# GpSimd's work on x, VectorE's order around the routing, and the order of eight experts in an encoder trunk

## The chip, the cores and the metric

The kernel runs on one core of a Trainium2 chip. The metric is device time in microseconds of one execution; the time before is the median of three runs. A core has TensorE (matmuls, and transposes as matmuls), VectorE, ScalarE, GpSimd and SyncE, which here issues most of the loads. They run their own instruction streams, each in order, and wait for one another by semaphores. In the profile they are PE, DVE, ACT, POOL and SP; PEld is TensorE's loading of the stationary operand, and a q behind a name is an engine's instruction queue.

## The reference, cut to what matters

```python
x = layer_norm(x, emb_ln_g, emb_ln_b)                     # x: 256 tokens x 1024, float32
for layer in range(2):
    m = mixer_block(x, ...)                               # projections, two kinds of attention, gates, output
    x = layer_norm(ALPHA * x + m, ln1_g[layer], ln1_b[layer])
    if layer == 0:
        f = swiglu(x, w_gate, w_up, w_down)               # dense, hidden width 2816
    else:                                                 # 8 experts, hidden width 3584, 2 per token
        logits = x @ w_router
        top_vals, top_idx = lax.top_k(logits, 2)
        top_w = softmax(top_vals)
        f = sum(combine[:, e:e+1] * swiglu(x, w_gate[e], w_up[e], w_down[e]) for e in range(8))
    x = layer_norm(ALPHA * x + f, ln2_g[layer], ln2_b[layer])
```

## The kernel before

**The dense part.** Activations stay on the chip, as two token tiles of 128 in `xt` and transposed in `xTh` and `xTl`. Weights come as tiles of 1 MB (`load_w`): SP issues the load into a `raw` buffer, ScalarE rounds it into `hi` (L185), VectorE subtracts to get `lo` (L192), and TensorE makes three matmuls of each product, high by high, low by high and high by low (L203 to L205). TensorE is fed from four `raw` buffers and four pairs of `hi` and `lo`.

**A seam.** Between two sub-layers a token tile is normalized (`ln_norm`, L225), transposed by TensorE and split again into high and low parts by VectorE (`to_xT`, L255 to L273); gain and bias are applied on the way to the transposed copy. The untransposed `xt`, which the next residual sum needs much later, gets its gain and bias from GpSimd (`ln_apply`, L234 and L237), in two multiplies and two adds of 1024 columns; the gain and then the bias are loaded as a broadcast into one buffer, tag `gb`. `rest` does the second token tile's transposition in the middle of the next sub-layer's first projection. In layer 0 `rest` gives back `end_norm`, the multiplies and adds for the embedding norm, called directly behind the first four projections.

**Routing.** `route(t)` is a generator in four parts for a token tile: (1) transposition, with ScalarE's high part `xth` and a low part `xtl` of the untransposed tile; (2) the router's logits; (3) ranks of the eight logits by comparisons on VectorE; (4) counts by matmul, giving each token's place (`pos`) in each expert. The router's weights `wr` stand in the `gb` buffer. `select` compares places with an iota to make a selection matrix `Sp`, and `gather` multiplies with it, on TensorE, to collect 128 token places of two experts at once into `gx`; ScalarE and VectorE copy the result out of PSUM. The second token tile's routing and the first pair's gather stand in a block in which only TensorE's order is fixed to the source's. GpSimd makes the second tile's `xtl`.

**The experts.** One at a time, in two halves of the hidden width: `gate_up` uses 16 tiles of 896 KB, `down` 7 tiles of 1 MB, raw float32, with TensorE in its 32-column blocks. A wide expert has 96 token places, a narrow one 64: three blocks or two. Down of one half runs behind gate and up of the next half; `scatter` adds an expert's weighted output to `xt`. The raw tiles rotate through 20 rooms (`rooms`), in program order. The first two experts are fixed (`FIXED = 2`, wide, loaded by constant addresses); the other six are sorted by their token counts on VectorE (`take_turns`) into the ranks of `RANK_AT`, the three largest wide, and SP reads the index from `who` ahead of an expert's loads (L1066). Experts are gathered in the pairs (0,1), (2,3), (4,5), (6,7), each pair at the end of the pair before. `cmi` (L845) says how far an expert's count goes past its places; every engine reads it into a register (L1121), and if it does, a loop at the end handles what is left over.

**What sets the order.** The program is put in order at build time by a list scheduler with its own times: on each engine the ready instruction that stands earliest in the code goes first, so later ones fill gaps. `manual_schedule(engines=...)` keeps the source's order on those engines. `issue_after(ins)` puts the instructions that its block traces on the engine of `ins` behind `ins` in issue order; it leaves other engines' instructions as they are and adds no wait for `ins` to finish. `hold_back` uses it for the next weights' splits. `warm(n)` issues n matmuls on constant data.

Of the kernel before, what the change touches and what calls it, by code (L numbers as in the profile page):

```python
# [15 lines left out]
AF = mybir.ActivationFunctionType  # L16
OP = mybir.AluOpType
# [48 lines left out]
def tile_encoder(ctx: ExitStack, tc: tile.TileContext, x_in, emb_g, emb_b, w_in, b_gate, na_rpb, sw_sink,  # L66
# [219 lines left out]
    def mixer(l, xh, xl, rest, x, mp, close_attention, early):  # L286
# [9 lines left out]
        def load_cols(c0, n):  # L296
            return [load_w(win[:, kh * 4:kh * 4 + 4, c0:c0 + n], 4, n) for kh in range(2)]
# [44 lines left out]
        if l == 0:  # L342
            with tc.manual_schedule(engines={PE, ACT, DVE}):
                end_norm = rest()
                wq = load_cols(1536, 512)
                for t in range(2):
                    proj_x(wkv, 256, t, ev_kv)
                for t in range(2):
                    proj_x(wq, 512, t, ev_q)
            end_norm()  # L350
            late_loads()
            nc.sync.dma_start(att, consts_in[:, :C_TRI])
        else:
            wq = load_cols(1536, 512)
            nc.sync.dma_start(att, consts_in[:, :C_TRI])
            for t in range(2):
                proj_x(wkv, 256, t, ev_kv)
                proj_x(wq, 512, t, ev_q, None if t else rest)
        wv = load_cols(1024, 512)
        for t in range(2):  # L360
            proj_x(wv, 512, t, ev_vna)

# [314 lines left out]
    def rest(ln, g, b):  # L677
        def part():
            out = to_xT(xt, ln, 1, *xT)
            if ln == 0:  # L680
                return lambda: ln_apply(xt, bcast(g, nc.sync), b, pool)
            hold_back(0, *out)
            ln_apply(xt, bcast(g), b, pool)
            return out[0]
        return part

# [2 lines left out]
    with tc.manual_schedule(engines={PE, ACT, DVE}):  # L689
        warm(12)  # L690
        second = ln_stats(xt[:, 1])
        to_xT(xt, 0, 0, *nxt, mid=lambda: ln_norm(xt[:, 1], second))
        warm(6)
    xT = list(nxt)
    with tc.tile_pool(name="mix0", bufs=1) as mp:
        mixer(0, *xT, rest(0, emb_g, emb_b), xt, mp, lambda ap: pools["att0"].close(), early(1))
# [25 lines left out]
    def route(t):  # L722

        tk = slice(t * 128, (t + 1) * 128)
        if not t:
            rt["xth"] = bp.tile([128, 2, D], F32R, tag="br0", name="xth")
            rt["xtl"] = bp.tile([128, 2, D], F32R, tag="br1", name="xtl")
            rt["xfull"] = xp.tile([128, KC, S], F32, tag="xTh", name="xfull")
        xth, xtl, xfull = rt["xth"], rt["xtl"], rt["xfull"]
        out = to_xT(xt, 3, t, None, None, full=xfull)  # L730
        with tc.issue_after(out.ins):
            rt[t] = act.activation(xth[:, t], xt[:, t], AF.Copy)
        (pool if t else dve).tensor_sub(xtl[:, t], xt[:, t], xth[:, t])
        yield

        ps = mm_bank()
# [2 lines left out]
            m = pe.matmul(ps[r, :128], rt["wr"][:, c], xfull[:, c, tk], start=c < 4, stop=c >= 4)  # L739
        lgT = part_tile([128, 128], "lgT")  # L740
        dve.tensor_copy(lgT, ps[:, :128])
        yield m
        ps = mm_bank()[:, :128]
        m = pe.transpose(ps, lgT, ident)
# [10 lines left out]
        dve.tensor_reduce(rank[:, t], gt, axis=AX.X, op=OP.add)  # L755
        dve.tensor_scalar(Ab[:, t], rank[:, t], 1.5, None, op0=OP.is_lt)
        dve.tensor_scalar(A[:, t], rank[:, t], 1.5, None, op0=OP.is_lt)
        yield m

        ps = mm_bank()  # L760
# [40 lines left out]

    FIXED = 2
    RANK_AT = [3, 0, 4, 1, 2, 5]
    WIDE = [True] * FIXED + [r < 3 for r in RANK_AT]

    def take_turns(comb):

# [38 lines left out]
    def gather(S_sel, n, bank=lambda c2: late_bank()):  # L848
# [15 lines left out]
        def out(c2):  # L864
            g, b = ln_col(3, 2 * c2)
            act.activation(gx[:, 2 * c2], pss[c2][:, 0], AF.Identity, bias=b, scale=g)
            g, b = ln_col(3, 2 * c2 + 1)
            dve.tensor_scalar(gx[:, 2 * c2 + 1], pss[c2][:, 1], g, b, op0=OP.mult, op1=OP.add)

        def step(c2):  # L870
            for t in range(2):
# [142 lines left out]

    def pair_select(Sp, pi, ts=(0, 1)):
        for i in range(2):
            e = 2 * pi + i
            src = turns[0] if turns else pos
            select(Sp, slice(i * 128, (i + 1) * 128), lambda t: src[:, t, e:e + 1], ts)

    def pair_start(pi):
        Sp = ep.tile([128, 2, 256], F32R, name="Sp")
        pair_select(Sp, pi)
        gx, steps, _ = gather(Sp, 256)
        return Sp, gx, steps

# [4 lines left out]

    Sp = ep.tile([128, 2, 256], F32R, name="Sp")
    gx, _, (gather_tile, gather_out) = gather(Sp, 256, acc_bank)
    with tc.manual_schedule(engines={PE}):
        steps = route(1)
        next(steps)
        next(routed)
        pair_select(Sp, 0, (0,))
        warm(4)
        next(steps)  # L1040
        gather_tile(0, 0)
        next(steps)
        for c2 in range(1, 4):
            gather_tile(c2, 0)
        warm(4)
        next(steps)
        warm(4)
        pair_select(Sp, 0, (1,))
        for c2 in range(KC // 2):
            gather_tile(c2, 1)  # L1050
            gather_out(c2)
    pair = Sp, gx, None
    ln_apply(xt, bcast(ln1_g[1]), ln1_b[1], pool)
    for t in range(2):
        pool.tensor_scalar(xt[:, t], xt[:, t], ALPHA, None, op0=OP.mult)
    new_pack()
    late = None
    ends = []
    for e in range(NE):
        Sp, gx, _ = pair  # L1060
        hs = slice(e % 2 * 128, e % 2 * 128 + 128)
        wide = WIDE[e]
        if e < FIXED:
            wg, wu, wd = mgv[:, e], muv[:, e], moe_d[0, e:e + 1]
# [5 lines left out]
        for j in range(LASTJ + 1):  # L1070
# [3 lines left out]
                    es.enter_context(tc.manual_schedule(engines={PE}))  # L1074
                h = gate_up(wg, wu, gx[:, :, hs], j, wide)
            if e == 0 and j == 1:
                comb = route_weights()
                turns += take_turns(comb)
            steps = []
            if j == LASTJ and e % 2 and e + 1 < NE:  # L1080
                pair = pair_start(e // 2 + 1)
                steps = pair[2]
            if j == 1 and ends:
# [117 lines left out]
```

## Time and profile before

| | |
|---|---|
| time before, median of 3 runs (lowest, highest) | 1434.43 us (1433.92, 1435.25) |
| the profiled execution's own time | 1437.59 us |
| its span, first to last instruction | 1435.8 us |
| busy share: TensorE, VectorE, ScalarE, GpSimd | 96%, 36%, 23%, 7% |
| mean granted clock of TensorE | 0.988 |
| bytes read from HBM | 448 MB, 313 GB/s over the span |
| GB/s in 40 slices, the first 16, then from the 18th to the 20th | 119 to 334, then 419, 419, 418 |

A timeline's row has the start and the length in us, the engine, the line, the operation, what is written from what is read with its shape, the count of merged instructions, and in brackets the idle time ahead of it and what ended it. A row of stretches has, for each engine, its busy time and (its instructions), then the granted clock as a share of 2.4 GHz, the DMA engines' busy share, and GB/s. All figures are of one execution.

### The profile page before, as it was taken

The numbers are of one execution on the slowest core, as the hardware profiler recorded it, in microseconds if no ns is written. First come the engines' busy times: TensorE is split into PE (matmuls) and PEld (weight loads), VectorE is DVE, ScalarE is ACT, GpSimd is POOL, SyncE is SP. The second block draws the span as 40 slices with busy tenths as digits, with TensorE's granted clock in tenths as the row PEclk, the third lists the DMA queues.
The fourth block names the chain that finished last, engine by engine and source line by source line (L and its number), as shares of the span: only waits on it lengthen the run. The fifth ranks groups of instructions, "written<-read, shape, count | busy, mean of one in ns | idle before, by whom it ended". The sixth has DMA issues, their size and how long they took to land. (4 is left out here: it accounts for less than half of the span.)

```text
span 1435.8 us, 26988 instructions
## 1 busy us (share of the span) xinstructions
PE 1380.6 (96%) x11875; PEld 774.8 (54%) x11875; DVE 511.5 (36%) x668; ACT 336.4 (23%) x533; POOL 100.6 (7%) x64
## 2 busy tenths in 40 slices
PE   7999999999999999899999999999999899999984
PEld 5888989999888897333333333333323233333321
DVE  8775686445677656611001101102010111101113
ACT  4566454444456653100000000000000000000000
POOL 4310030000050100500000000000000000000000
PEclk8999999999999999999999999999999999999998
DMA  8744456554474387599999999999999999999993
GB/s 292 221 131 138 153 166 228 186 195 163 152 228 145 119 334 282 205 419 419 418 405 356 374 419 417 419 420 418 418 420 418 419 419 418 419 419 419 418 419 145
DMA packets 122858, 451.24 MB, mean 314 GB/s; under 512 B 8032, under 2 KB 57568, under 8 KB 108528
## 3 DMA queue, kind: packets, MB, share of 16 engines
q1 hardware_dynamic: 120768, 442.91, 79.4%
q0 software_dynamic: 1968, 6.55, 1.6%
q8 instruction: 95, 1.56, 0.4%
q14 instruction: 27, 0.22, 0.0%
HBM read 448.38 MB, written 1.05 MB: 313 GB/s over the span
## 5 line engine op out<-in xcount | busy, mean ns | idle before, releaser
L933 PE MATMUL mm<-raw,gx 128*32 128x448 f32 x3648 | 370.2, 540 | 0.9 <-DMA raw<-in_moe_w_gate_dram 0.6
L933 PEld LDWEIGHTS mm<-raw,gx 128*32 128x32 f32 x3648 | 117.2, 110 | 224.7 <-issue 207.7
L192 DVE TENSOR_TENSOR lo<-raw,hi 128x2048 fp32r<-128x2048 f32 (+1 forms) x85 | 203.7, 2400 | 93.8 <-ACT hi L185 93.5
L962 PE MATMUL a<-raw,hT 128*32 128x512 f32 x1680 | 197.5, 594 | 12.3 <-DMA raw<-in_moe_w_down_dram 12.2
L203 PE MATMUL mm<-xTh,hi 128*128 128x256 f32 x704 | 202.3, 287 | 0.0
L205 PE MATMUL mm<-xTh,lo 128*128 128x256 f32 x704 | 200.0, 284 | 0.0
L204 PE MATMUL mm<-xTl,hi 128*128 128x256 f32 x704 | 199.6, 284 | 0.0
L933 PE MATMUL a<-raw,gx 128*32 128x448 f32 x1728 | 187.2, 540 | 0.0
L185 ACT ACTIVATE hi<-raw 128x2048 fp32r<-128x2048 f32 (+1 forms) x85 | 158.7, 1873 | 77.6 <-PE mm L204 43.2
L203 PEld LDWEIGHTS mm<-xTh,hi 128*128 128x128 f32 x704 | 134.6, 191 | 7.2 <-issue 5.4
L205 PEld LDWEIGHTS mm<-xTh,lo 128*128 128x128 f32 x704 | 134.6, 191 | 3.1 <-issue 3.1
L204 PEld LDWEIGHTS mm<-xTl,hi 128*128 128x128 f32 x704 | 134.7, 191 | 1.9 <-issue 1.5
L938 DVE TENSOR_TENSOR h<-h,mm 128x448 f32<-128x448 f32 x32 | 19.9, 621 | 303.2 <-PE mm L933 300.6
L962 PEld LDWEIGHTS a<-raw,hT 128*32 128x32 f32 x1680 | 50.8, 110 | 136.4 <-issue 102.7
L933 PEld LDWEIGHTS a<-raw,gx 128*32 128x32 f32 x1728 | 55.4, 110 | 107.5 <-issue 103.5
L937 ACT ACTIVATE h<-mm 128x448 f32<-128x448 f32 x25 | 13.6, 544 | 319.6 <-PE mm L933 319.6
L967 PE MATMUL a<-raw,hT 128*32 128x512 f32 x560 | 72.8, 592 | 0.0
L945 DVE STREAM_TRANSPOSE hT<-h 128x1344 f32<-128x1344 f32 (+1 forms) x15 | 33.6, 2240 | 106.0 <-PE a L967 54.0
L976 ACT ACTIVATE y<-a 128x512 f32<-128x512 f32 x8 | 4.8, 597 | 271.0 <-PE a L962 271.0
L1116 POOL DMA_DIRECT2D raw<-in_ln_g_dram x1 | 0.6, 602 | 774.9 <-PE mm L933 774.9
L205 PE MATMUL mm<-hi,xTl 128*128 128x256 f32 (+1 forms) x128 | 44.8, 351 | 3.4 <-DVE xTl L273 3.4
L203 PE MATMUL mm<-hi,xTh 128*128 128x256 f32 (+1 forms) x128 | 45.4, 357 | 2.3 <-DVE xTh L272 2.3
(243 smaller groups left out, 1420.6 us busy)
## 6 DMA issues: line engine op xcount, KB each, us to landing
raw<-in_moe_w_gate_dram SPq DMA_DIRECT2D x128, 896.0 KB, 17.7
raw<-in_moe_w_up_dram SPq DMA_DIRECT2D x128, 896.0 KB, 17.4
raw<-in_moe_w_down_dram SPq DMA_DIRECT2D x111, 1024.0 KB, 18.6
raw<-in_w_in_dram SPq DMA_DIRECT2D x32, 1024.0 KB, 6.4
raw<-in_ffn_w_gate_dram SPq DMA_DIRECT2D x11, 1024.0 KB, 5.4
raw<-in_ffn_w_up_dram SPq DMA_DIRECT2D x11, 1024.0 KB, 5.5
raw<-in_ffn_w_down_dram SPq DMA_DIRECT2D x11, 1024.0 KB, 5.1
raw<-in_w_out_dram SPq DMA_DIRECT2D x8, 1024.0 KB, 5.9
```

Of the source, the lines that this page charges most:

```text
L185: act.activation(hi[:, p], raw[:, p], AF.Copy)
L192: eng.tensor_sub(lo[:, p], raw[:, p], hi[:, p])
L203: pe.matmul(o, lh, rh, start=first, stop=False)
L204: pe.matmul(o, lh, rl, start=False, stop=False)
L205: pe.matmul(o, ll, rh, start=False, stop=last)
L933: pe.matmul(out[q * 32:q * 32 + 32], gx[:, c, s * 32:s * 32 + 32], wt[:, q * Q:(q + 1) * Q], start=c == 0, stop=c == KC - 1)
L937: act.activation(h[:, s, 0:Q], banks[0][s], AF.Silu)
L938: dve.tensor_mul(h[:, s, 0:Q], h[:, s, 0:Q], banks[1][s])
L945: dve.transpose(hT, h.rearrange("p s (f b) -> p s b f", f=32))
L962: pe.matmul(yb[0][r:r + 32], hT[s][:, m], w[:, n * 512:(n + 1) * 512], start=first, stop=last)
L967: pe.matmul(yb[1][r:r + 32], hT[2][:, m - 1 + i], wt[:, i, n * 512:(n + 1) * 512], start=j == 0 and m == 1, stop=last)
L976: act.activation(y[:, 0], yb[0], AF.Copy)
```

## The change

- `end_norm()` moves behind the issue of the value projection's weight loads, and so behind the loads of three constants; the warm-up there grows from 6 to 13 matmuls.
- At the seams' `ln_apply`, and at the one after the routing together with the multiplication by ALPHA, an `issue_after` is put, named after a VectorE instruction.
- In `route(1)` ScalarE's high part comes ahead of the transposition, and the low part is VectorE's in two halves, one behind the logits' copy and one behind the ranks. The block around it fixes VectorE's order as well. The warm-up ahead of the counts goes from 4 matmuls to 1.
- `FIXED` is 1, seven experts go by rank, the four largest wide. The order of widths becomes wide, narrow, wide, wide, wide, narrow, wide, narrow (before: wide, wide, narrow, wide, narrow, wide, wide, narrow). The gathered pairs become (0,0), (1,2), (3,4), (5,6), (7,7), one more than before, each gathered in an even expert's second half.
- `route_weights` and `take_turns` are put behind the last copy of the gather on VectorE.

```diff
@@ mixer
-            end_norm()
             late_loads()
...
         wv = load_cols(1024, 512)
+        if l == 0:
+            end_norm()
@@ rest
-            ln_apply(xt, bcast(g), b, pool)
+            with tc.issue_after(out[1].ins):
+                ln_apply(xt, bcast(g), b, pool)
@@
-        warm(6)
+        warm(13)
@@ route
+        def low_part(n):
+            ns = slice(n * 512, (n + 1) * 512)
+            dve.tensor_sub(xtl[:, t, ns], xt[:, t, ns], xth[:, t, ns])
+
+        if t:
+            act.activation(xth[:, t], xt[:, t], AF.Copy)
         out = to_xT(xt, 3, t, None, None, full=xfull)
-        with tc.issue_after(out.ins):
-            rt[t] = act.activation(xth[:, t], xt[:, t], AF.Copy)
-        (pool if t else dve).tensor_sub(xtl[:, t], xt[:, t], xth[:, t])
+        if not t:
+            with tc.issue_after(out.ins):
+                act.activation(xth[:, t], xt[:, t], AF.Copy)
+            low_part(0)
+            low_part(1)
...
         dve.tensor_copy(lgT, ps[:, :128])
+        if t:
+            low_part(0)
...
         dve.tensor_scalar(A[:, t], rank[:, t], 1.5, None, op0=OP.is_lt)
+        if t:
+            low_part(1)
@@
-    FIXED = 2
-    RANK_AT = [3, 0, 4, 1, 2, 5]
-    WIDE = [True] * FIXED + [r < 3 for r in RANK_AT]
+    FIXED = 1
+    RANK_AT = [4, 0, 1, 2, 5, 3, 6]
+    WIDE = [True] * FIXED + [r < 4 for r in RANK_AT]
@@ pair_select
-            e = 2 * pi + i
+            e = min(max(2 * pi - 1 + i, 0), NE - 1)
@@ the block of the second token tile
-    with tc.manual_schedule(engines={PE}):
+    with tc.manual_schedule(engines={PE, DVE}):
...
-        warm(4)
+        warm(1)
...
-            gather_out(c2)
+            gathered = gather_out(c2)
     pair = Sp, gx, None
-    ln_apply(xt, bcast(ln1_g[1]), ln1_b[1], pool)
-    for t in range(2):
-        pool.tensor_scalar(xt[:, t], xt[:, t], ALPHA, None, op0=OP.mult)
+    with tc.issue_after(gathered.ins):
+        ln_apply(xt, bcast(ln1_g[1]), ln1_b[1], pool)
+        for t in range(2):
+            pool.tensor_scalar(xt[:, t], xt[:, t], ALPHA, None, op0=OP.mult)
...
-        hs = slice(e % 2 * 128, e % 2 * 128 + 128)
+        hs = slice((e + 1) % 2 * 128, (e + 1) % 2 * 128 + 128)
...
-                comb = route_weights()
-                turns += take_turns(comb)
+                with tc.issue_after(gathered.ins):
+                    comb = route_weights()
+                    turns += take_turns(comb)
...
-            if j == LASTJ and e % 2 and e + 1 < NE:
+            if j == LASTJ and e % 2 == 0 and e + 1 < NE:
                 pair = pair_start(e // 2 + 1)
```

## Rows read from the trace of the kernel before

**Rows 1.** Stretches: busy time of PE, PEld, DVE, ACT, POOL; clock, DMA share, GB/s.
```profile
18.00:30.00 12.00, 8.67 (x38) 7.28 (x37) 11.49 (x6) 5.96 (x8) 8.37 (x5) 0.72 0.77 271
...
580.00:600.00 20.00, 16.05 (x140) 7.45 (x144) 17.75 (x52) 4.81 (x7) 14.40 (x7) 0.83 0.33 102
720.00:740.00 20.00, 20.00 (x200) 6.33 (x196) 3.10 (x2) 0.60 (x1) 0.00 (x0) 1.00 1.00 394
760.00:820.00 60.00, 60.00 (x567) 21.74 (x560) 11.14 (x19) 3.35 (x6) 0.00 (x0) 1.00 0.93 354
840.00:860.00 20.00, 20.00 (x220) 6.94 (x216) 2.11 (x2) 1.09 (x2) 0.00 (x0) 1.00 1.02 420
```

**Rows 2.** Timeline of TensorE, the last expert's down projection.
```profile
1390.54 1.92 PE L962 MATMUL a<-raw,hT 128*32 128x512 f32 x16 [0.56 <-DMA raw<-in_moe_w_down_dram]
...
1412.92 3.64 PE L962 MATMUL a<-raw 128*32 128x512 f32 x32 [0.56 <-SPq L1122]
```

**Rows 3.** Timeline of SP, the first expert's loads around its start.
```profile
591.02 0.33 SPq L199 DMA_DIRECT2D raw<-in_moe_w_gate_dram  x1
...
596.94 1.29 SPq L199 DMA_DIRECT2D raw<-in_moe_w_gate_dram  x3
```

**Rows 4.** Waits of SP, 575 to 600: us in total, times, longest.
```profile
SPq L1121 <- DVE cmi L845: 4.7, 1, 4.7
```

**Rows 5.** Timeline of TensorE: gather, first expert's start; down with gather, and without.
```profile
583.95 0.55 PE L861 MATMUL a<-Sp,xth 128*128 128x256 f32 x1 [4.25 <-DVE turn_v L830]
...
587.63 1.72 PE L933 MATMUL mm<-raw,gx 128*32 128x448 f32 x8
...
771.63 1.92 PE L962 MATMUL a<-raw,hT 128*32 128x512 f32 x16
...
787.07 1.92 PE L962 MATMUL a<-raw,hT 128*32 128x512 f32 x16
...
789.67 1.90 PE L962 MATMUL a<-raw,hT 128*32 128x512 f32 x16
```

**Rows 6.** Timeline of VectorE: routing, and the first expert's two products.
```profile
573.83 0.48 DVE L880 TENSOR_SCALAR Sp<-cst,pos 128x128 fp32r<-128x128 f32 x2
...
575.49 2.08 DVE L751 TENSOR_TENSOR eq<-lg 128x64 f32<-128x64 f32 x1
...
578.46 0.16 DVE L757 TENSOR_SCALAR A<-rank 128x8 f32<-128x8 f32 x1
...
581.18 2.62 DVE L880 TENSOR_SCALAR Sp<-cst,pos 128x128 fp32r<-128x128 f32 x2
...
598.38 0.27 DVE L839 CAST who<-turn_at 128x6 int32<-128x6 f32 x1
623.42 2.12 DVE L938 TENSOR_TENSOR h<-h,mm 128x448 f32<-128x448 f32 x3 [24.76 <-PE mm L933]
...
659.50 2.13 DVE L938 TENSOR_TENSOR h<-h,mm 128x448 f32<-128x448 f32 x3 [31.39 <-PE mm L933]
```

**Rows 7.** Timeline of GpSimd: the embedding norm's multiplies, and the routing.
```profile
17.95 5.14 POOL L234 TENSOR_TENSOR x<-x,gb 128x1024 f32<-128x1024 f32 x2 [17.02 <-DMA gb<-in_emb_ln_g_dram]
...
574.50 0.57 POOL L229 DMA_DIRECT2D gb<-in_ln_g_dram  x1 [6.13 <-PE mm L739]
575.08 2.39 POOL L733 TENSOR_TENSOR xtl<-x,xth 128x1024 fp32r<-128x1024 f32 x1
578.88 4.64 POOL L234 TENSOR_TENSOR x<-x,gb 128x1024 f32<-128x1024 f32 x2 [1.41 <-DMA gb<-in_ln_g_dram]
```

**Rows 8.** Timeline of VectorE in the first seam.
```profile
18.01 2.85 DVE L273 TENSOR_TENSOR xTl<-xTf,xTh 128x512 fp32r<-128x512 f32 x1
...
24.01 4.49 DVE L192 TENSOR_TENSOR lo<-raw,hi 128x2048 fp32r<-128x2048 f32 x2
```

**Rows 9.** One tile, `att`: its load in layer 0, issue and time to landing.
```profile
L352 SPq DMA_DIRECT2D att<-in_consts_dram x1: 430/430/430, 9.5 to 9.5; - x1
...
DMA to landing us min/median/max: 10.6/10.6/10.6
```

More of the change, by code (lines that the diff above doesn't have):

```diff
@@ L867, in out @@
             g, b = ln_col(3, 2 * c2 + 1)
-            dve.tensor_scalar(gx[:, 2 * c2 + 1], pss[c2][:, 1], g, b, op0=OP.mult, op1=OP.add)
+            return dve.tensor_scalar(gx[:, 2 * c2 + 1], pss[c2][:, 1], g, b, op0=OP.mult, op1=OP.add)
         def step(c2):
```

## Prediction

> **What bounds the kernel now.** I read three views. First the stretches: in the expert stage TensorE shows busy all the time and the DMA engines move 420 GB/s, so one of the two only looks busy. The last expert decides: TensorE stands still 0.56 us before each pair of down-projection blocks, waiting for its weights, ten times in a row from 1390.54 to 1412.92 [rows 1, 2]. So the end is the arrival of the last weight tile plus a fixed tail (1435.8 - 1413 = 23 us), and before that every microsecond in which the DMA engines idle in the expert stage is lost. The stretches show where they idle, against 419 GB/s: 580-600 at 102 GB/s loses 20 x (1 - 102/419) = 15.1 us, 720-740 at 394 loses 1.2, 760-820 at 354 loses 9.3: together 25.6 us [rows 1]. Ahead of 580 TensorE is the bound; its stalls are in the seams between sub-layers.
>
> The Trainium skill (Perfetto Trace Analysis, Identifying the Most-Contended Engine) says that matmul busy time is a bad measure of a TensorE bound and that weight-load time should be read beside it. The row of 840-860 has weight loads at 6.94 of 20 us, so by that rule too TensorE is not at its peak there; read by matmul busy time alone the sum would be that of the first rival.
>
> Why the first gap: the prefetch has filled its 20 tile rooms by 569 us and SP issues the 21st weight load at 591.02, when the first expert has used up a tile, and the next only at 596.94 [rows 3], because SP was queued for 4.7 us behind a register load of `cmi`, the overflow count [rows 4]. The first expert in turn started at 587.63, after a token gather that waited 4.25 us for VectorE and then ran at the lower clock (16 matmuls in 3.68 us; 580-600 has a granted clock of 0.83) [rows 1, 5]. The second gap, 760-820, is the end of two wide experts in a row: their scatter and the next pair's gather add TensorE work while all rooms are full.
>
> **The change, part by part.**
>
> (1) `issue_after` around `ln_apply` and the later scale. It puts into order only instructions on the engine of the instruction named, and adds no wait; named is a VectorE instruction, inside are GpSimd ones. I cost these at 0: GpSimd's order stays. The bounds: if it did take hold, -1.3 us (TensorE's small stalls of about 0.6 us in each of two seams) to +1.
>
> (2) Order of the second token tile's routing. Before, GpSimd's subtraction of the low part began at 575.08 and VectorE's next comparison took 2.08 us, where such small ones take some 0.2; then, with GpSimd's multiply from 578.88 on, VectorE ran a side product before the two selections, and those took 2.62 us for 0.48 [rows 6, 7]. After, the subtraction is VectorE's (two of 0.7), nothing of GpSimd's runs until the multiply, and that cannot start before the gain vector has landed, whose buffer is the router's and whose load is issued after the logits (574.50, landing 4.4 us later) [rows 7]. Chain: logits a bit later since ScalarE copies first (+0.2); comparison at 575.7 instead of 575.49; the rank result ends at 578.62 - 1.9 (the stall) + 0.2 = 576.9; second low part to 577.6; position 577.75; both selections by 578.25, ahead of the multiply at 578.9 by 0.65 us. The gather starts at 578.3 with TensorE just warmed, its 16 matmuls at the full clock take some 1.9, and the first expert starts at 580.3 instead of 587.63: **7.3 us earlier**.
>
> (3) Expert order and the DMA stream. Of a wide expert a half takes 36.1 us of gate and up (from 623.42 to 659.50, 16 tiles of 2.255 us) [rows 6] and 7 down pairs of 2.60 us, 18.2 [rows 5]: 108.6 us in all, against 46 tiles at 0.957 MB/0.419 = 2.285 us = 105 us of transfer. A narrow one has two thirds, 72.4. So wide experts let the rooms fill, narrow ones empty them. Before: wide, wide, narrow, wide, narrow, wide, wide, narrow. After: wide, narrow, wide, wide, wide, narrow, wide, narrow; five wide in both. The pairs for the gather shift by one, which adds a fourth gather: 771.63 to 787.07 is four pairs with a gather step each, 15.44 - 4 x 2.60 = 5.0 us of TensorE [rows 5].
>
> DMA idle after 580, term by term. The 21st load goes out at 580.3 + 3.4 (591.02 less 587.63) = 583.7; less the 1.3 us in which the prefetch's last bytes still land after 580 (the first row counts them too), **2.4**. During the first expert loads go out at TensorE's pace, 2.255 us for a tile of 0.9175 MB, 407 GB/s, which loses 3% of 90 us = 2.7, and the gather now lies in its first down: 5.0, of which some 2.7 are covered by the two tiles in flight: **5.0**. SP's register load stays queued among the weight loads. VectorE's 44 small routing instructions start at 581 right behind the gather, and share the time to about 593 with GpSimd; SP may wait, but three loads are out by 588 and the stream, faster than TensorE, makes most of it good: **0.5** (0 to 7, the last if it waits as long as before with one load out). Then the narrow expert: 83 us of TensorE (with scatters) for 46 tiles that take 106: rooms are free 28 us ahead (4.8 at its start). The three wide experts with two gathers and the scatters take 341 us for 138 tiles that take 318; 22 of the 28 are used up, 6 are left, about as much as a load takes to land: **1** (0 to 6). Sum 8.9 against 25.6: **16.7 us saved**, the earlier start of part 2 included.
>
> (4) `who`, the table of ranks, was ready at 598.4 [rows 6] and is first needed for the 47th tile, now the second expert's, which gets a room when the 27th is used up, at 580.3 + 27 x 2.255 = 641. 0, with 43 us of cover. Selection of the pair: likewise.
>
> (5) First seam. GpSimd's multiplies, 17.95 to 23.09 [rows 7], made VectorE's step at 18.01 last 2.85 us, and the next one likewise [rows 8], TensorE stood still 3.3 us of 18-30 and ran with a clock of 0.72 there [rows 1]. After, the gain load sits behind three constants on SP instead of ahead of them; I take SP to issue it before the value weights, which have no buffer until 12 us, so that it lands about when the last of the three did, 9.5 + 10.6 = 20.1 [rows 9]. VectorE's steps are then done (18.65, 19.05, 19.7) and its first weight split has begun (2.2 us each [rows 8]) and ends at 22.0; TensorE's next projection starts then, and not behind the first split's old end, 24.01 + 2.2 = 26.2. Of its 48 matmuls of 512 columns (some 10.5 us at 2.4 GHz) the second block waits for the second split, which GpSimd holds to 26.6, 1.9 us; before they lost as much to the clock, half the speed from 26.2 to nearly 30. So 26.2 - 22.0 = **4.2 us**, from which I take 0.2 for a clock drop that may remain: **4.0**. Bounds: 0 (it lands at 18.7, and the same two steps are hit) to 6.3 (it goes out behind the value weights and hits neither). Seven more warm-up matmuls lie in TensorE's idle time: 0 (at best -0.6).
>
> The Trainium skill (SBUF — State Buffer, SBUF: two separate sides) has the port pair that VectorE and GpSimd share as a lock held for the whole instruction by whoever starts first. The stretched rows agree with the loser waiting out an instruction; taken strictly, a split that has begun holds GpSimd back and the first seam gives the 4.2; GpSimd starting at 18.7, it gives 0.
>
> **Sum.** The profiled execution took 1437.6 us (span 1435.8 and 1.8 around it). 1437.6 - 16.7 - 4.0 = 1416.9; the median of the runs is 1434.4, 3.2 lower, so **1413.7 us**.
>
> **Rivals.** A: TensorE sets the end of the expert stage, and idle DMA there costs nothing. For it: busy without a gap in 760-820 [rows 1]. Against: it waits for weights throughout the last expert [rows 2]. It would give 4.0 + 7.3 - 5.0 (fourth gather) = 6.3: 1428.1.
> B: the selections still meet GpSimd's multiply (margin 0.65 us), both held, 4.6 us, and the clock falls before the gather, 0.9: 5.5 less, 1419.2. For it: the margin is smaller than the error of the chain. Against: the load's 4.4 us is the time with the DMA engines busy, as they will be.
> C: the three wide experts in a row fill the rooms again and SP's wait stays: 6 + 6.5 - 1.5 = 11 less, 1424.7. For it: 6 us of slack in a sum of 341.
> D, slower than before: `cmi` comes late, in SP's queue. The chain that computes it stands in the code behind the first expert's second half; if it sits on VectorE behind the products of the first half (623.42 before, 616.1 after [rows 6]), `cmi` is ready at 616.1 + 2.1 + 44 x 0.16 = 625, and SP, which has its register load ahead of the fourth weight load or so, sends nothing from 588 till then. Of that some 5 us are made good, 32 are not, as the transfers are the bound: 1446. It decides from a `cmi` later than 593 + 21 = 614 on. For it: this wait is there already [rows 4], and the whole chain now starts behind the gather. Against: the chain stood behind the same code before and was done at 598.4.
> E: the change does what part 1 denies, GpSimd's waits take hold: part 1's 1.3, 1412.4; told from the forecast only by the trace.
>
> **How the numbers follow.** Forecast 0.55 (own range 1408 to 1419), E 0.05, B 0.12, C 0.10, A 0.08, D 0.06, nothing of it measurable 0.04. The range runs from 1407.5 (the first seam's best and no idle from part 3's doubtful terms) to 1428 (C, and A at its edge). What a measurement of this kernel can tell from no change is about 0.2%, 2.9 us: faster takes forecast, E, A, B and C, 0.90; same 0.04; slower 0.06.
>
> **What would show it.** First expert's first matmul 11 us earlier in the trace (4.0 + 7.3); the selections at 0.48 us; GpSimd's multiplies at the middle seams where they were (else E); DMA at 419 GB/s in every stretch after the first expert (a dip in the fifth expert is C); TensorE waiting for weights in the last expert (else A); the load of `cmi` on SP under 5 us of wait. I am wrong if the first expert starts less than 5 us earlier or if the dips move rather than go.

## The result, and the profile after the change

The changed kernel takes 1418.97 us (median of 4 executions, 1418.82 to 1420.44), the kernel before 1434.84 in the same job: a ratio of 0.9891, 95% interval 0.988 to 0.9903. The forecast was 1413.7, in a range of 1407.5 to 1428.0, faster with a chance of 0.90. The direction held and the range holds the time; the gain of 15.9 us is 4.8 less than the 20.7 that was forecast, and the time 5.3 above the forecast one. The profiled execution took 1418.82 us (span 1416.9), 18.8 less than the profiled one of before.

I read the trace of the changed kernel in the order of the prediction. First TensorE, VectorE and GpSimd in the first seam.

```profile
21.39 0.39 PE L203 MATMUL mm<-hi,xTh 128*128 128x512 f32 x1
...
26.32 0.50 PE L204 MATMUL mm<-lo,xTh 128*128 128x512 f32 x1 [1.39 <-DVE lo L192]
```
```profile
17.91 0.69 DVE L273 TENSOR_TENSOR xTl<-xTf,xTh 128x512 fp32r<-128x512 f32 x1
18.52 0.42 DVE L272 CAST xTh<-xTf 128x512 fp32r<-128x512 f32 x1
...
19.58 13.30 DVE L192 TENSOR_TENSOR lo<-raw,hi 128x2048 fp32r<-128x2048 f32 x4
```
The cast in the kernel before:
```profile
20.78 2.59 DVE L272 CAST xTh<-xTf 128x512 fp32r<-128x512 f32 x1
```
GpSimd in the changed kernel:
```profile
20.59 7.93 POOL L234 TENSOR_TENSOR x<-x,gb 128x1024 f32<-128x1024 f32 x2 [3.48 <-DMA gb<-in_emb_ln_g_dram]
```

The step of 2.85 us [rows 8] takes 0.69, and the cast behind it 0.42 for 2.59. GpSimd's multiplies start at 20.59 (forecast: 20.1) and meet the weight splits instead: four take 13.30 us, 3.3 each, where they took 2.2 undisturbed [rows 8]. TensorE's first 512-column matmul stands at 21.39 and not at 26.45, its second block waits 1.39.

Then the routing, on the same three engines.

```profile
573.63 0.39 PE L875 MATMUL a<-Sp,xth 128*128 128x256 f32 x1 [0.16 <-DVE Sp L894]
...
575.73 0.96 PE L947 MATMUL mm<-raw,gx 128*32 128x448 f32 x8
```
```profile
570.00 0.29 DVE L751 COPY lgT<-mm 128x128 f32<-128x128 f32 x1
570.21 0.68 DVE L734 TENSOR_TENSOR xtl<-x,xth 128x512 fp32r<-128x512 f32 x1
...
573.09 0.48 DVE L894 TENSOR_SCALAR Sp<-cst,pos 128x128 fp32r<-128x128 f32 x2
575.06 1.91 DVE L882 TENSOR_SCALAR gx<-a,pcol 128x256 f32<-128x256 f32 x4 [1.49 <-ACT gx L880]
576.89 2.36 DVE L800 TENSOR_SCALAR oh<-rank 128x16 f32<-128x16 f32 x2
```
```profile
570.28 0.56 POOL L229 DMA_DIRECT2D gb<-in_ln_g_dram  x1 [6.28 <-PE mm L749]
574.43 4.71 POOL L234 TENSOR_TENSOR x<-x,gb 128x1024 f32<-128x1024 f32 x2 [3.59 <-DMA gb<-in_ln_g_dram]
```

The two selections take 0.48 us together, not 2.62 [rows 6], and are done 0.9 us ahead of GpSimd's multiply. The gather waits 0.16 us and not 4.25, and its 16 matmuls run at 2.4 GHz (granted clock 1.00 from 560 to 580), 2.1 us to the first expert where 3.68 were needed [rows 5]. That expert starts at 575.73, 11.9 us earlier.

Last the weight stream: stretches (columns as in [rows 1]), SP's issues, its one wait for a register, and TensorE in the last expert's down projection.

```profile
18.00:30.00 12.00, 10.30 (x53) 8.34 (x54) 11.97 (x6) 7.37 (x9) 8.68 (x3) 1.00 0.91 307
580.00:600.00 20.00, 20.00 (x220) 6.97 (x216) 5.27 (x44) 3.12 (x5) 10.37 (x5) 1.00 0.99 390
600.00:620.00 20.00, 20.00 (x220) 6.92 (x216) 4.36 (x4) 0.00 (x0) 0.00 (x0) 1.00 1.01 420
660.00:680.00 20.00, 20.00 (x196) 7.08 (x192) 5.47 (x10) 0.80 (x2) 0.00 (x0) 1.00 0.91 338
760.00:820.00 60.00, 60.00 (x628) 20.24 (x624) 4.36 (x4) 2.77 (x5) 0.00 (x0) 1.00 1.02 418
1080.00:1100.00 20.00, 20.00 (x180) 7.59 (x176) 6.78 (x12) 1.13 (x2) 0.00 (x0) 1.00 0.98 379
```
```profile
578.35 0.33 SPq L199 DMA_DIRECT2D raw<-in_moe_w_gate_dram  x1
...
580.60 0.33 SPq L199 DMA_DIRECT2D raw<-in_moe_w_gate_dram  x1
...
583.93 0.33 SPq L199 DMA_DIRECT2D raw<-in_moe_w_gate_dram  x1
```
```profile
SPq L1138 <- DVE comb L813: 2.4, 1, 2.4
```
```profile
1378.77 1.92 PE L976 MATMUL a<-raw,hT 128*32 128x512 f32 x16 [0.56 <-DMA raw<-in_moe_w_down_dram]
```

The dip of 760 to 820 is gone. Two small ones came where the forecast put them: in the first expert's down projection, with the gather (338 GB/s), and in the third of the three wide experts in a row (379). SP's wait for the overflow count is 2.4 us and not 4.7. TensorE waits for weights in the last expert's down projection, as before.

For all kernels of this study I use three numbers of the trace: where the first expert's first matmul stands, how long it is from there to the end, and the idle of the DMA engines in it. The idle is summed over stretches up to 800 us behind the start, length x (1 - GB/s / 419). The runs named e1 to e12 are told below.

| kernel | median us (executions) | first expert at | from there to the end | DMA idle in it |
|---|---|---|---|---|
| before | 1434.84 (4) | 587.63 | 848.2 | 19.8 |
| before, again (e5) | 1433.78 (1) | 584.11 | 847.9 | 19.3 |
| first seam alone (e1) | 1434.42 (12) | 582.18 | 848.5 | 20.8 |
| routing alone (e2) | 1425.80 (5) | 579.27 | 846.4 | 17.7 |
| order of experts alone (e3) | 1428.82 (6) | 584.39 | 841.9 | 14.9 |
| changed | 1418.97 (4) | 575.73 | 841.2 | 12.9 |
| without `issue_after` (e4) | 1417.59 (4) | 575.08 | 841.2 | 13.1 |
| low part on GpSimd (e7) | 1418.27 (4) | 575.27 | 841.0 | 12.8 |
| no three wide in a row (e8) | 1417.78 (6) | 574.58 | 840.7 | 10.8 |
| changed, again (e9) | 1417.77 (5) | 574.57 | 840.7 | 12.8 |
| gain loaded later (e10) | 1416.37 (5) | 573.62 | 840.8 | 12.8 |
| gather of one expert (e11) | 1417.55 (5) | 575.12 | 840.6 | 12.5 |
| combined (e12) | 1415.35 (5) | 572.83 | 840.3 | 9.9 |

From before to changed 11.9 us come ahead of the first expert and 7.0 behind it, and the idle fell by 6.9. That the last two agree so closely is partly chance, since the idle up to 800 us leaves out two things of about one size. Behind the start the changed kernel also moves 0.5 MB of bias for GpSimd, some 1.2 us of the stream, which before landed ahead of the start (part 3 below); and the last stretch of its stream, behind the 800 us, idles some 1.8 us less (e8). Counted up to the last weight the idle is 25.0 us before and 16.4 in the changed kernel.

### The profile page after: what moved, and what is told of

Read it like the earlier page. It is cut to its first block, busy times and chain, and to the rows that moved or that the text cites. A ratio compares the mean times of both kernels' runs of the same rounds, so it can differ in the third digit from the quotient of the medians.

```text
span 1416.9 us, 27180 instructions
## 1 busy us (share of the span) xinstructions
PE 1379.5 (97%) x11911; PEld 776.0 (55%) x11911; DVE 504.9 (36%) x680; ACT 338.7 (24%) x537; POOL 98.9 (7%) x63
## 5 line engine op out<-in xcount | busy, mean ns | idle before, releaser
L947 PE MATMUL a<-raw,gx 128*32 128x448 f32 x1664 | 174.6, 539 | 0.0
L204 PE MATMUL mm<-lo,xTh 128*128 128x256 f32 (+1 forms) x128 | 43.8, 342 | 1.5 <-DVE lo L192 1.4
## 6 DMA issues: line engine op xcount, KB each, us to landing
raw<-in_moe_w_down_dram SPq DMA_DIRECT2D x111, 1024.0 KB, 18.6
```

Of the source, the lines that this page charges most:

```text
L204: pe.matmul(o, lh, rl, start=False, stop=False)
L947: pe.matmul(out[q * 32:q * 32 + 32], gx[:, c, s * 32:s * 32 + 32], wt[:, q * Q:(q + 1) * Q], start=c == 0, stop=c == KC - 1)
```

## The experiments

**e1 to e3: one part at a time, on the kernel before.** They ran in one job, beside 17 executions of the kernel before (median 1436.21, 1434.1 to 1440.9).

e1, the first seam:

```diff
-            end_norm()
             late_loads()
...
         wv = load_cols(1024, 512)
+        if l == 0:
+            end_norm()
...
-        warm(6)
+        warm(13)
```

> The kernel before with the move of the embedding norm and the longer warm-up alone. Theory: TensorE sets the pace from the first seam to the first expert, so the 4.2 us by which its first 512-column projection starts earlier (measured in the trace of the whole change, 5.1 there less 1.4 of a new stall and so on) reach the end: 4.2 us less than before. Rival: a later wait of the dense part, or the weight stream of the experts, takes it back: 0 to 2 us less.

Measured: 1434.42 us, ratio 0.9988 (0.9973 to 1.0002), 1.8 us less and not clear of zero. The trace shows the seam as in the changed kernel, but the twelve times fell into two groups, 1430.6 to 1432.5 and 1436.4 to 1438.6. Inconclusive on the sum. In the profiles of this kernel (e1, e6) the first expert starts at 582.2 and 582.3, 1.8 to 5.5 us earlier than in the two of the kernel before, and 848.5 us follow, as before: the seam's gain does reach the first expert, and its size hangs on which execution of the kernel before it is held against.

e2, the routing:

```diff
+        if t:
+            act.activation(xth[:, t], xt[:, t], AF.Copy)
         out = to_xT(xt, 3, t, None, None, full=xfull)
...
-        (pool if t else dve).tensor_sub(xtl[:, t], xt[:, t], xth[:, t])
...
+        if t:
+            low_part(0)
...
+        if t:
+            low_part(1)
...
-    with tc.manual_schedule(engines={PE}):
+    with tc.manual_schedule(engines={PE, DVE}):
```

(`low_part` subtracts one half on VectorE; with the warm-up of 1 and `route_weights` behind the gather, as in the change)

> The kernel before with the new order of the second token tile's routing alone (low part on VectorE in two halves, VectorE's order fixed, shorter warm-up, route weights behind the gather), old expert order. Theory (the weight stream sets the end): the first expert starts 7.7 us earlier, and as the overflow count is ready sooner, of the 8.8 us in which the DMA engines idle in the first 15 us of the first expert about 3.6 go too: 11.3 us less. Rival (TensorE sets the end): 7.7 us less, whatever the DMA engines do behind the start.

Measured: 1425.80, ratio 0.9926 (0.9913 to 0.9939): 10.4 less, nearer to 11.3 than to 7.7. From the second tile's logit copy to the first expert it is 5.74 us, against 13.40 before. Behind that start 1.8 us were gained, not 3.6: the idle of the first 15 us fell by 3.3, and some of it came back, 0.4 in the dip at the end of the two wide experts and 0.5 from 75 to 120 us behind the start. That a stream which is further ahead finds the rooms full sooner would explain it; no run shows it.

e3, the order:

```diff
-    FIXED = 2
-    RANK_AT = [3, 0, 4, 1, 2, 5]
-    WIDE = [True] * FIXED + [r < 3 for r in RANK_AT]
+    FIXED = 1
+    RANK_AT = [4, 0, 1, 2, 5, 3, 6]
+    WIDE = [True] * FIXED + [r < 4 for r in RANK_AT]
```

(with the shifted pairs)

> The kernel before with the new order of experts, the shifted pairs and seven ranks alone. Theory (the weight stream sets the end): the 10.5 us of idle DMA between 120 and 220 us behind the first expert's start go, 4.8 come in the first expert's down projection with its gather and 1.9 in the three wide experts in a row: 3.7 us less. Rival (TensorE sets the end): the fourth gather's 5.0 us are added: 5 us more than before.

Measured: 1428.82, ratio 0.9955 (0.9941 to 0.9968): 7.4 less. The rival in which TensorE sets the end wanted 5 more and is out. In the traces it is 6.0 behind the start against e5, more than the 3.7 expected: the fourth gather's dip is 3.2 here and not 4.8, it seems because the stream, started late, has not filled the rooms by then. The idle up to 800 us fell by 4.4; the rest lies in the stream's last stretch, which idles some 1.8 us less here (e8). Stretches of e3:

```profile
660.00:680.00 20.00, 20.00 (x176) 8.20 (x172) 2.96 (x8) 2.26 (x4) 0.00 (x0) 1.00 0.94 369
760.00:820.00 60.00, 60.00 (x610) 20.16 (x606) 8.35 (x10) 2.23 (x4) 0.00 (x0) 1.00 1.01 419
1090.00:1110.00 20.00, 20.00 (x176) 7.64 (x176) 6.78 (x12) 1.13 (x2) 0.00 (x0) 1.00 0.98 378
```

The three parts add to 19.6 us; the whole gave 18.6 in that job (e4, below).

**e4: does `issue_after` do anything around GpSimd's work?**

```diff
-            with tc.issue_after(out[1].ins):
-                ln_apply(xt, bcast(g), b, pool)
+            ln_apply(xt, bcast(g), b, pool)
...
-    with tc.issue_after(gathered.ins):
-        ln_apply(xt, bcast(ln1_g[1]), ln1_b[1], pool)
+    ln_apply(xt, bcast(ln1_g[1]), ln1_b[1], pool)
```

> The changed kernel without the two issue_after around GpSimd's multiplies and adds. Theory: they order only VectorE's instructions, of which there are none inside, so nothing changes: 0 against the changed kernel, and GpSimd's multiplies in the two middle seams stand where they stood. Rival: they hold GpSimd back, and without them the two middle seams cost 1.3 us more.

Measured: 1417.59 us; with and without the two lines each of the five engines has the same instructions in the same order. So GpSimd's work does not wait for the VectorE instruction that is named: behind the routing it starts when its gain vector lands. Rival E is out.

**e5, e6: how much does the first seam vary?** No edit.

> The kernel before, profiled once more. Theory: the execution profiled at first lay 3.2 us above the median because its first seam (TensorE's two stops of 3.3 us and the low clock behind them) was an unlucky one; in another execution the first 512-column projection starts between 24 and 26 us instead of 26.45, with less time at the low clock, and the rest of the trace agrees within 1 us. Rival: the 3.2 us lie anywhere, or in the profiler, and the first seam is as it was: 26.4 us.

Measured: one execution of 1433.78 us, span 1432.0, 3.8 shorter than the first profiled one. VectorE, then TensorE, in its first seam, and the stretch:

```profile
16.81 2.90 DVE L273 TENSOR_TENSOR xTl<-xTf,xTh 128x512 fp32r<-128x512 f32 x1
19.63 2.59 DVE L272 CAST xTh<-xTf 128x512 fp32r<-128x512 f32 x1
```
```profile
25.31 0.53 PE L203 MATMUL mm<-hi,xTh 128*128 128x512 f32 x1
```
```profile
18.00:30.00 12.00, 9.18 (x43) 7.96 (x44) 11.49 (x6) 5.51 (x7) 8.58 (x6) 0.86 0.85 299
```

The same two steps are hit, a little over a microsecond earlier, and behind the two stops TensorE runs at 1.2 GHz until 25.3 and not until near 30 (0.86 granted in 18 to 30, against 0.72 [rows 1]). TensorE reaches the transposes of the next sub-layer at 187.56 us, against 190.08: 2.5 of the 3.8 us lie in the first seam, 0.9 more between there and 562 us. The theory holds for the larger part.

> The kernel before with the move of the embedding norm alone, profiled once more: its times fell into two groups, 1430.6 to 1432.5 and 1436.4 to 1438.6 us. Theory: the first seam is the same in both (first 512-column projection at 21.4 us), and the 6 us lie in the old routing or behind it, where GpSimd's work meets VectorE's by chance. Rival: the first seam itself has two states, one at 21.4 us and one some 6 us later. A profile in the upper group tells them apart; in the lower group it only repeats the first one.

Measured: 1432.53 us, in the lower group again, first expert at 582.30, all as in e1. The upper group was not caught. In each of the three jobs of experiments the kernel before had such executions too, some 5 us above the rest (3 of 17, 2 of 11, 6 of 9), and e3 had one; the 43 executions of kernels with the new routing had none (in no kernel more than 2.8 us between the lowest and the highest). So it belongs to the old routing or hangs on it; where it sits is open.

**e7: is it VectorE making the low part that helps?**

```diff
-            dve.tensor_sub(xtl[:, t, ns], xt[:, t, ns], xth[:, t, ns])
+            (pool if t else dve).tensor_sub(xtl[:, t, ns], xt[:, t, ns], xth[:, t, ns])
```

> The changed kernel with the low part of the second token tile made by GpSimd again, in two halves; all else as changed. Theory: GpSimd's subtraction falls on VectorE's comparisons again and stretches one of them to some 2 us, as before; the first expert starts 2.0 us later than in the changed kernel and the whole takes 2.0 us more. Rival: VectorE saves its two subtractions of 0.68 us and the start is 1 us earlier; or the order of VectorE alone gave the gain and nothing changes.

Measured: 1418.27 us: nothing lost, within what a kernel varies from job to job (1417.6 to 1419.0 for the changed one). GpSimd, then VectorE:

```profile
566.97 2.49 POOL L734 TENSOR_TENSOR xtl<-x,xth 128x512 fp32r<-128x512 f32 x2 [3.98 <-ACT xth L737]
569.40 0.58 POOL L229 DMA_DIRECT2D gb<-in_ln_g_dram  x1
573.42 4.72 POOL L234 TENSOR_TENSOR x<-x,gb 128x1024 f32<-128x1024 f32 x2 [3.43 <-DMA gb<-in_ln_g_dram]
```
```profile
568.45 1.29 DVE L894 TENSOR_SCALAR Sp<-cst,pos 128x128 fp32r<-128x128 f32 x2
...
572.62 0.48 DVE L894 TENSOR_SCALAR Sp<-cst,pos 128x128 fp32r<-128x128 f32 x2
```

My expectation missed. Since ScalarE's high part now comes ahead of the transposition, GpSimd's subtraction runs before the comparisons and is over at 569.5; it stretches the first tile's selections by 0.8 us, and the way from the second tile's transposes to the first expert grows by 0.5 (9.43 for 8.88), no more. What counts is that the subtraction is over ahead of the comparisons and the selections ahead of the multiply, not which engine subtracts. Whether ScalarE's new place or VectorE's fixed order brings that about, no run tells apart: both stand in e2 and in e7.

**e8: no three wide experts in a row.**

```diff
-    RANK_AT = [4, 0, 1, 2, 5, 3, 6]
+    RANK_AT = [4, 0, 1, 5, 2, 3, 6]
```

> The changed kernel with the order of widths wide, narrow, wide, wide, narrow, wide, wide, narrow, so no three wide experts in a row. Theory (rooms full in the third wide expert): the dip of DMA at 500 to 540 us behind the first expert's start, 1.9 us of idle, goes, and no other comes: 1.9 us less than the changed kernel. Rival: the dip moves to the second pair of wide experts, or another wait takes it: 0.

Measured: 1417.78 us, against 1417.59 (e4) and 1417.77 (e9): nothing. Yet the dip is gone and the idle is 2.0 us less. The last stretches of the stream, of the changed kernel and then of e8, show where it went:

```profile
1380.00:1384.00 4.00, 2.77 (x28) 0.65 (x24) 0.00 (x0) 0.00 (x0) 0.00 (x0) 1.00 1.01 418
1384.00:1388.00 4.00, 3.54 (x32) 0.68 (x25) 0.00 (x0) 0.00 (x0) 0.00 (x0) 1.00 1.01 417
1388.00:1392.00 4.00, 2.86 (x28) 0.70 (x28) 0.00 (x0) 0.00 (x0) 0.00 (x0) 1.00 0.68 278
1392.00:1396.00 4.00, 3.45 (x36) 0.81 (x28) 0.00 (x0) 0.00 (x0) 0.00 (x0) 1.00 0.41 166
```
```profile
1380.00:1384.00 4.00, 3.36 (x32) 0.92 (x32) 0.00 (x0) 0.00 (x0) 0.00 (x0) 1.00 0.91 372
1384.00:1388.00 4.00, 2.99 (x32) 0.70 (x28) 0.00 (x0) 0.00 (x0) 0.00 (x0) 1.00 0.59 243
1388.00:1392.00 4.00, 3.27 (x32) 0.55 (x21) 0.00 (x0) 0.00 (x0) 0.00 (x0) 1.00 0.55 221
1392.00:1396.00 4.00, 3.60 (x32) 0.91 (x32) 0.00 (x0) 0.00 (x0) 0.00 (x0) 1.00 0.22 88
```

At the end the DMA engines fall to some 225 GB/s at a busy share near 0.55, for about 6 us in the changed kernel and 11 in e8, and TensorE's last block of weights starts 818 us behind the first expert in both. The rival's outcome, then, but for a reason neither had named: some of the 16 engines are done while others still carry their share, and the slowest sets the end. The trace shows it, though no view prints it: every weight load reports its landing in 16 parts. In the changed kernel the first and the last part of a load lie 7.0 us apart (median of 40 us) ahead of the dip at 500 us behind the start, 3.6 behind it and 6.8 at the end. In e8, without that dip, they go on from 6.8 to 11.6. So in a dip the engines that are ahead stand still and the late ones catch up, and taking the dip away gives time only to those that had time to spare: counted up to the last weight, the idle is 16.4 us in the changed kernel and 16.3 in e8. At the end of the changed kernel seven of the 16 parts of a load land within 1.2 us and the other nine 3 to 7 us behind the first: nine of 16 is the busy share of 0.56.

It is not the number of dips that sets the length of this end but how long ago the last one was. The kernel before idled most of all (19.8 us), but its last dip is at 180 to 220 us behind the start: its parts end 10.4 us apart, and its half-rate end is some 9 us. In e3, with a last dip where the changed kernel has it, they are 6.7 and 6 us.

**e9 to e12: three more edits.** One job, with the changed kernel as their measure.

> The changed kernel once more, beside the three that follow, as their measure. Theory: within 0.1% of its first time (1419 us), first expert at 575 to 576 us, and TensorE's 1.4 us stop at the second weight split of the first seam again. Rival: the first seam varies as it did before the change, by 1 to 3 us from one execution to the next.

Measured: 1417.77 us, first expert at 574.57, the stop of 1.39 us again. The changed kernel varies by 1.2 us between jobs.

e10, the gain behind the value weights on SP (`loads[-1]` is their second load):

```diff
         if l == 0:
-            end_norm()
+            with tc.issue_after(loads[-1].ins):
+                end_norm()
```

> The changed kernel with the embedding norm's gain loaded behind the two value weight tiles on SP, so that GpSimd's multiplies start some 3 to 5 us later, behind the second weight split. Theory: TensorE's stop of 1.4 us in its first 512-column projection goes and reaches the end: 1.4 us less than the changed kernel. Rival: the multiplies meet the third and fourth split or the rotary products instead and TensorE stops there, or the gain lands as early as before: 0.

Measured: 1416.37 us, 1.4 less than e9, as expected, but not clear of the noise: the two sets of five overlap (1415.4 to 1418.2 and 1417.2 to 1418.5), and in the two profiles the first expert starts 0.95 earlier and as much time follows. GpSimd's multiplies start at 26.22 and TensorE has no stop left there:

```profile
26.22 6.67 POOL L236 TENSOR_TENSOR x<-x,gb 128x1024 f32<-128x1024 f32 x2 [9.31 <-DVE lo L194]
```

e11, gathering one expert in the first expert's down:

```diff
-            if j == LASTJ and e % 2 == 0 and e + 1 < NE:
+            if j == LASTJ and e == 0:
+                Sp = ep.tile([128, 2, 256], F32R, name="Sp")
+                select(Sp, slice(0, 128), lambda t: turns[0][:, t, 1:2])
+                gx, steps, _ = gather(Sp[:, :, 0:128], 128)
+                pair = Sp, gx, None
+            if j == LASTJ and e % 2 and e + 1 < NE:
                 pair = pair_start(e // 2 + 1)
```

> The changed kernel, where the first expert's second half gathers the second expert alone (128 columns and not 256), and the pairs (2,3), (4,5), (6,7) are gathered in experts 1, 3 and 5. Theory (average idle of the DMA engines counts): the gather in the first expert's down costs 2.5 us and not 5.0, the dip of DMA behind it is 2.4 us of idle and not 4.8, and the whole takes 2.4 us less. Rival (the end of the stream is set by the slowest of the 16 DMA engines, which goes on working in a short dip, as the run without three wide experts in a row suggests: 2.1 us less idle, nothing gained, a half-rate end of 12 us and not 6): less than 0.8 us, and the half-rate end grows by the rest.

Measured: 1417.55 us, nothing. It does not tell the two apart, since the gather did not get shorter. Groups of TensorE, changed kernel and then e11:

```profile
L875 PE MATMUL a<-Sp,xtl 128*128 128x256 f32 x8 | 2.0, 280 | 0.0
```
```profile
L875 PE MATMUL a<-Sp,xtl 128*128 128x128 f32 x8 | 1.9, 274 | 0.0
```

Half the columns save 6 ns of 280 a matmul; they start 0.11 us apart and not 0.12.

e12, the edits of e8, e10 and e11 together, and the register load of the overflow count behind the 61st weight load (`sent[60]`):

```diff
-    cnt = nc.values_load(cmi[0:1, 0:1], min_val=0, max_val=S)
+    with tc.issue_after(sent[60].ins):
+        cnt = nc.values_load(cmi[0:1, 0:1], min_val=0, max_val=S)
```

> The changed kernel with the three edits together (gain load behind the value weights, single gather, no three wide experts in a row), and SP's register load of the overflow count put behind the 61st weight load. Theory: 1.4 + 2.4 + 0 to 1 us less than the changed kernel, 4 us. Rival (slowest DMA engine): 1.4 from the first seam and under 1.5 from the rest.

Measured: 1415.35 us (1414.88 to 1416.07), 2.4 less than e9 with no overlap, and the fastest kernel here; ratio to before 0.9833 (0.9813 to 0.9854) in that job, where e9 has 0.985 (0.983 to 0.9871). Both ratios flatter the change, since six of the nine executions of the kernel before were of the upper group there. Of the 2.4, 1.7 lie ahead of the first expert and 0.4 behind it, though the idle fell by 2.9: the slowest engine again (the half-rate end is some 11 us here). SP has no wait for the count any more, and the idle of the first 10 us is 5.3 us, as in e9 (5.1): that wait cost nothing.

## Why the prediction was right, and 5 us off

**Part 1, `issue_after` at 0: right** (e4).

**Part 2, first expert 7.3 us earlier: right,** 7.7 from the logit copy to the first expert. The selections' lead was 0.9 us (forecast 0.65), so rival B did not come. One reason was wrong: the subtraction need not be VectorE's (e7, where the way to the first expert grows by 0.5 us). In the prediction both the subtraction's collision and its engine changed in one step; what mattered was when it runs. And the selections' 2.62 us are not the fixed price of the old order that the prediction took them for. VectorE in e3, whose routing is the old one:

```profile
578.11 2.06 DVE L787 TENSOR_TENSOR rt_tmp<-oh,lg 128x16 f32<-128x16 f32 x1
...
580.09 0.47 DVE L880 TENSOR_SCALAR Sp<-cst,pos 128x128 fp32r<-128x128 f32 x2
```

Here the selections take 0.47 us, and two side products ahead of them 2.28 and 2.06. Which step the multiply stretches varies; the sum does not, since from the logit copy to the first expert it is 13.2 to 13.6 us in all five profiles with the old routing. What the change removes is their meeting with the multiply.

The Trainium skill (SBUF — State Buffer, SBUF: two separate sides) names as VectorE's contenders for the shared ports its instructions in a two-port mode and those with two inputs from SBUF. The rows agree in that the copies out of PSUM, 1.91 us for four, run beside GpSimd's multiply from 574.43 on as they do everywhere in this trace (0.53 to 0.55 us each), while the next one, which reads SBUF, takes 2.36 for two; no row shows which mode that one runs in.

**Part 3, 9.4 us behind the start (16.7 less 7.3): too much, 7.0 came.** The sum of idle was forecast at 8.9 and measured at 12.9. Term by term: the first expert's pace and gather 5.0, measured 4.8; `cmi` 0.5, measured 0 (e12); three wide in a row 1, measured 1.9; the restart 2.4, measured 5.2; the rest, 1.0, is spread thin. The 5.0 came out by luck: it was 2.7 for the pace of the first expert's loads and 2.3 for the gather, and the pace cost 0.2 (420 GB/s from 600 to 620, not 407) and the gather's dip 4.8.

The mis-sized term is the restart. I subtracted 1.3 us of prefetch that lands after 580 before the change, and that was a misreading: no weight lands there between 578 and the load of 591.02, and the bytes of 584 to 588 are GpSimd's load of the bias. Stretches of the kernel before, and GpSimd:

```profile
580.00:582.00 2.00, 0.00 (x0) 0.00 (x0) 2.00 (x2) 0.00 (x0) 2.00 (x2) 1.00 0.00 0
...
586.00:588.00 2.00, 2.00 (x12) 1.61 (x15) 1.77 (x8) 1.54 (x4) 0.00 (x0) 0.50 0.55 197
```
```profile
583.95 0.68 POOL L229 DMA_DIRECT2D gb<-in_ln_b_dram  x1 [0.42 <-POOL x L234]
588.43 4.70 POOL L237 TENSOR_TENSOR x<-x,gb 128x1024 f32<-128x1024 f32 x2 [3.81 <-DMA gb<-in_ln_b_dram]
```

Stretches of the changed kernel around the start:

```profile
574.00:576.00 2.00, 2.00 (x20) 1.75 (x22) 0.94 (x3) 1.53 (x4) 1.57 (x1) 1.00 0.04 8
576.00:578.00 2.00, 2.00 (x24) 0.54 (x20) 2.00 (x4) 1.68 (x2) 2.00 (x2) 1.00 0.00 0
578.00:580.00 2.00, 2.00 (x27) 0.67 (x23) 2.00 (x10) 0.00 (x0) 1.58 (x2) 1.00 0.38 61
580.00:582.00 2.00, 2.00 (x28) 0.76 (x24) 2.00 (x24) 0.88 (x2) 0.17 (x1) 1.00 0.87 315
```

Nothing of the prefetch lands behind the start here either, and the bias, issued at 579.57, now lands among the first weights. The 21st load goes out 2.6 us behind the start, sooner than the 3.4 that I took; but I had left out that a load issued at 578.35 moves its first bytes near 579.7 (an estimate: 61 GB/s over 2 us are 0.3 us of transfer), and that the full rate comes only later (315 GB/s from 580 to 582). The account by idle DMA comes out for this change, in part by chance; it fails where the slack is in single engines (e8, e12), and rival C, which wanted full rooms to bring the old loss back, had the place right and the price too high.

**Part 4, `who` at 0: right;** the table is ready at 585.5 us.

**Part 5, first seam 4.0: right,** 4.5 at the transposes of the next sub-layer between the two profiled executions (190.08 to 185.62), 3.6 between the means of four executions with the old seam (188.6) and eight with the new one (185.0).

**The sum: its last step failed.** "The median of the runs is 1434.4, 3.2 lower" took the profiled execution's excess for something that stays. It sat, for the most part, in the first seam (e5), and so in a term that the change removes: it was counted as saved and then taken off a second time. The profiled execution of the changed kernel lies at its own median. Against the profiled time the forecast was 1416.9 and 1418.8 came, 1.9 off: 2.4 too much in part 3, 0.6 too little in parts 2 and 5. The other 3.2 of the 5.3 are that step.

## What to carry to other kernels

A time that a profile shows above the median is somewhere in that profile: profile the same kernel again before carrying the difference on, above all when the change removes a stall that depends on when a load lands. Where a stream from HBM sets the end, count its idle time first, but look at its last stretch too: if it ends at half rate, some DMA engines are done before others, a short dip lets the late ones catch up, and taking it away may buy nothing. And when two engines collide, ask first whether the work can be done at another time; which engine does it may not matter. A term of a forecast that comes out right is still to be taken apart: the 5.0 of part 3 held two errors that cancelled.

## What the runs showed of the hardware

- The weight stream runs at 418 to 420 GB/s with all 16 DMA engines busy, and ends at some 225 GB/s and a busy share of 0.56. This end is the longer, the longer ago the last dip was: 6 us where that lies 500 to 520 us behind the first expert's start (changed, e3), 9 at 180 to 220 (before, e1, e2), 11 at 80 to 105 (e8, e12).
- The 16 parts in which a load lands drift apart while the stream runs without a pause: from 3.6 to 6.8 us between the first and the last in the 300 us behind the changed kernel's last dip, and from 6.8 on to 11.6 in e8, which lacks that dip. A dip of 1.9 us of mean idle took them from 7.0 back to 3.6.
- A gather matmul with 128 columns costs nearly what one with 256 does (0.11 and 0.12 us from start to start): beside each stands a weight load of 0.19 us.
- VectorE's copies out of PSUM took their usual 0.53 to 0.55 us beside GpSimd's multiply, where steps on SBUF of some 0.2 us took up to 2.4.
